# Another place for the keys' and values' group among five gate groups, and context rows eighteen pieces apart

## The chip, the cores and the metric

The kernel runs on one core of one Trainium2 chip. Its engines each have a queue of their own and work through it in order: TensorE (PE) multiplies matrices, VectorE (DVE) and ScalarE (ACT) do arithmetic by element, GpSimd (POOL) does small work and issues DMAs that add to what lies at their target, and SyncE (SP) issues most loads. Engines wait for each other, and for transfers, by semaphores. The metric is device time in microseconds (us), the median of several runs.

## The reference, cut to what matters

One layer of an attention and Fourier block on 512 tokens of width 2048 in float32, with 256 tokens of context. Nearly all time goes into one projection of width 9216 and the output products behind it.

```python
h  = _modulate(_rmsnorm(xs, norm_g[l]), shift[:, None], scale[:, None])   # 512 x 2048
hc = _modulate(_rmsnorm(cs, norm_g[l]), shift_c, scale_c)                 # 256 x 2048
pc_kv = hc @ w_l[:, OFF_K:OFF_ZA]                  # keys and values of the context
kc = _rmsnorm(_heads(pc_kv, 0, N_KV_HEADS), k_norm_g[l])
vc = _heads(pc_kv, KV_W, N_KV_HEADS)
p = h @ w_l                                        # q, k, v, z_a, u_b, z_b, g_a, g_b
q = _rope(_rmsnorm(_heads(p, OFF_Q, N_Q_HEADS), q_norm_g[l]), cos, sin) * q_scale
k = _rope(_rmsnorm(_heads(p, OFF_K, N_KV_HEADS), k_norm_g[l]), cos, sin)
v = _heads(p, OFF_V, N_KV_HEADS)
attn = _attention(q, jnp.concatenate([k, kc], axis=1), jnp.concatenate([v, vc], axis=1))
y = _merge(p[..., OFF_ZA:], attn, w_proj_a[l], w_proj_b[l], w_out[l])
#   in _merge:  y_a = (attn * silu(z_a)) @ w_pa,  y_b = (fourier(u_b) * silu(z_b)) @ w_pb
#               (sigmoid(g_a) * y_a + sigmoid(g_b) * y_b) @ w_out
out = _rmsnorm(xs + gate[:, None] * y, final_g)
```

## The kernel before, in words

**Groups.** Eight groups of 1024 columns of the projection run one after the other: three groups of queries and z (`qz`), two gate groups, the group of the keys and values (`kv`, number `KV` = 5), two more gate groups. The gate groups compute the sigmoids of g_a and g_b and store them (L813, L814). The list `KINDS` names them, and the host lays the columns of `w_g` out in that order. The keys' group also multiplies the context, so it is longer than the others. After the eighth group come attention, the two branch projections and the output projection.

**Products and pieces.** Each group is computed as a two by two block product in Winograd's manner, with seven products in place of eight, in the order P1, Q5, P2, Q6, P7, Q3, Q4. A product has four pieces (P2.0 to P2.3). A piece is 128 x 1024 raw weights (512 KB). To keep float32's precision every factor is split in a high and a low part: `hi` is a copy rounded by ACT (L163), `lo` is the difference formed by DVE (L164). Three matmuls (L305 to L307: hi by hi, hi by lo, lo by hi) replace one, which gives twelve matmuls of 512 columns for each piece.

**Sums of weights.** Products Q5, Q6, and Q4 need sums of the four quarters of a group's weights, piece by piece. Four buffers R0 to R3, one for each piece, hold them: SP loads the first quarter (L205), DVE adds the second for Q5 (L250), and POOL issues DMAs that add the third and the fourth (L261), each as soon as the split that reads the buffer is done. P7 needs the sum less a quarter, which DVE subtracts into the raw buffer (L252) in the time of the products ahead.

**Buffers.** Raw weights are loaded (L202) into four buffers of one pool and up to two more (`raw0`, `raw1`). Split weights go into three pairs of `hi`, `lo`, and two more pairs on the place of x's halves (their rows read `s33`, `s35`, `s63`, `s65`, and so on, in halves of 512 columns), which are given up for the end of the group ahead of the keys' and come back in the group behind it. From the seventh group on two further raw buffers, `gvp`, open where `qr` lay. `qr` holds what the rotation and transposition of queries and keys (L860 to L872) writes, the stores of the queries (L899, `q_d`) and of the keys (L912, `k_d`) read, and the context's rows use in between. L215 loads queries back for attention.

**Context.** The context's norm is formed in the first gate group: `context_spread` needs L987. Then its rows are normalised, modulated and brought into the seven forms of the products in four blocks (L1002 to L1011, then ACT, then a store, `cr` pieces). Each block takes one raw buffer, and stands at a fixed place in the sequence of pieces, counted from the first gate group.

**Order.** The program is written in the order of the products, a piece splits several pieces ahead, and pieces are loaded as far ahead as buffers allow. A scheduler then orders each engine's queue by when it deems work ready. Thus a change of places in the lists also changes which of two instructions stands first on DVE or SP.

Of the kernel before, what the change touches and what calls it, by code (L numbers as in the profile page):

```python
# [33 lines left out]
O_Q, O_K, O_V, O_ZA, O_UB, O_ZB, O_GA, O_GB, IN_W = 0, 1536, 2048, 2560, 4096, 4608, 5120, 7168, 9216  # L34
# [20 lines left out]
BY_DVE_GATES, BY_DVE_OUT = (1,), ()  # L55


KINDS = ("qz", "qz", "qz", "gate", "gate", "kv", "gate", "gate")
NQZ, KV = 3, 5
LAST = len(KINDS) - 1  # L60

CTX_FORMS = ("A11", "Z5", "A12", "A22", "S3", "S2", "S4")
# [2 lines left out]
def context_piece(g, name, pc):  # L65

    n = 28 * (g - NQZ) + 4 * ONE_GROUP.index(name) + pc
    if n % 2 == 0 and 0 <= n < 8:
        return "cn", n // 2
    if n % 10 == 4 and 14 <= n < 54:  # L70
        return "cr", n // 10 - 1

# [33 lines left out]
def block_kernel(ctx, tc, xT, ctx_rows, ctx_toks, x, c_row, w_ss, w_gate, vecs, qkg, rope, dft_c, dft_s,  # L108
# [4 lines left out]
    def region(name, side="left", **kw):  # L113
        st = ExitStack()
        return st, st.enter_context(tc.tile_pool(name=name, bufs=1, side=side, **kw))
# [596 lines left out]
    def job():  # L712
        if late:
            late.pop(0)()
        if jobs:
            jobs.pop(0)()
# [93 lines left out]
    def gate_done(half, c, v, t):  # L810
        t = new_ev() if t is None else t
        g = KINDS[: group.g].count("gate")
        nc.scalar.activation(t, v, ACT.Sigmoid)  # L813
# [8 lines left out]
    def load_rotations(rows):  # L822
        nc.scalar.dma_start(turning, rope)
        nc.scalar.dma_start(new_q()[:, 0, 0:2, :], rows)

    def rotations(factor):
        r, gq = turning, new_q()[:, 0, 0:2, :]
        for a in range(2):
            nc.vector.scalar_tensor_tensor(r[:, a], r[:, a], factor,
                                           gq[:, None, a, :].broadcast_to([P, 4, HD]), op0=ALU.mult, op1=ALU.mult)  # L830
# [213 lines left out]
    qz, qs, kv = {}, {}, {}  # L1044

    def load_head(h):
        qz[h] = take((2, T))
        nc.gpsimd.dma_start(qz[h][:, 1, :], flat(z_d[h]))
        load_turned(qz[h][:, 0, :], q_d[h // 4], h % 4)

    def get_keys(g):
        keys = get(("K", g))
        kv[g] = tuple(w[:, 0, :] for w in keys) + get(("V", g))

    def split_queries(h):
        qs[h] = take((2, T), F32R)
        split_from(qz[h][:, 0, :], qs[h][:, 0, :], qs[h][:, 1, :])

    load_rotations(qkg[:, 0:2, :])
    for g, kind in enumerate(KINDS):  # L1060
        if g == 3:
            jobs += [lambda: None] * 8 + [context_norm, lambda: None, lambda: None, context_spread]
        elif g == KV:
            while jobs:
                job()
            assert not any(p[2] == "raw1" for e in ahead for p, _ in e.raws)
        elif g == KV + 1:
            hl_pools += range(MORE_HL)
        group = Group(g, forms, new_ev, {"qz": qz_done, "kv": kv_done, "gate": gate_done}[kind], {"a": "x", "b": "y", "c": "x"})
        if g == KV:  # L1070
            group.more = Context()
        for name in ONE_GROUP:
            if (g, name) == (0, "Q5"):
                hl_pools += range(MORE_HL)
                rotations(HD ** -0.5)
            elif (g, name) == (KV, "P1"):
                load_rotations(qkg[:, 2:4, :])
            elif (g, name) == (KV, "Q5"):
                rotations(1.0)
            elif (g, name) == (KV - 1, "Q3"):  # L1080
                raw_pools.remove((rp, 1, "raw1", 1))
                hl_pools[:] = [p for p in hl_pools if not isinstance(p, int)]
            elif (g, name) == (KV + 1, "Q6"):
                qzs.close()
                gvs, gvp = region("gvp", "right", reuse_waits="tile")
                raw_pools += [(rp, 1, "raw1", 1), (gvp, 2, "raw", 2)]
            elif (g, name) == (LAST, "P7"):
                raw_pools.pop()
                raw_pools.remove((rp, 1, "raw1", 1))
            elif (g, name) == (LAST, "Q3"):  # L1090

                free += [(fms[i], f"s{i}") for i in (4, 5, 6, 7, 12, 13, 14, 15, 8, 9, 10, 11, 2, 3, 0, 1)]
                for h in range(2):
                    load_head(h)
            elif (g, name) == (LAST, "Q4"):
                hl_pools[:] = [p for p in hl_pools if not isinstance(p, int)]
                get_keys(0)
                jobs.append(lambda: split_queries(0))
            group.run(name)
# [429 lines left out]
def _constants():  # L1529
    pos = np.arange(T)  # L1530
    inv = (THETA ** (-np.arange(32, dtype=np.float64) / 32)).astype(np.float32)
    ang = np.stack([(pos // GRID).astype(np.float32)[:, None] * inv,
                    (pos % GRID).astype(np.float32)[:, None] * inv], axis=1)
    ang = ang.astype(np.float64)
    cos, sin = np.cos(ang), np.sin(ang)
    cos = np.stack([cos, cos], axis=2).reshape(T, HD)
    sin = np.stack([-sin, sin], axis=2).reshape(T, HD)
    rope = np.stack([cos, sin]).reshape(2, 4, P, HD).transpose(2, 0, 1, 3).astype(np.float32)
    a = 2 * np.pi * (np.outer(np.arange(P), np.arange(P)) % P) / P
    dft_c = np.concatenate([np.cos(a), -np.sin(a)], axis=1).astype(np.float32)  # L1540

    f = np.concatenate([np.arange(0, T, 2), np.arange(1, T, 2)])
    a = 2 * np.pi * (np.outer(np.arange(T // 2), f) % T) / T
    dft_s = np.stack([np.cos(a), np.sin(a)]).reshape(2, 2, P, T).transpose(2, 0, 1, 3).reshape(P, 2, 2 * T).astype(np.float32)
    return np.ascontiguousarray(rope), np.ascontiguousarray(dft_c), np.ascontiguousarray(dft_s)


def _layout(x, c, ctx, c_ctx, w_ada, b_ada, norm_g, w_in, q_norm_g, k_norm_g, w_proj_a, w_proj_b, w_out, final_g):
    A = lambda v: np.ascontiguousarray(v)
    x, ctx, w_ada, w_in = (np.asarray(v)[0] for v in (x, ctx, w_ada, w_in))  # L1550
    w_pa, w_pb, w_o = (np.asarray(v)[0] for v in (w_proj_a, w_proj_b, w_out))
    col = lambda v: np.asarray(v).reshape(KK, P).T
    rope, dft_c, dft_s = _constants()
    d = {}
    d["xT"] = A(x.T.reshape(KK, P, T).transpose(1, 0, 2))

    d["ctx_rows"] = A(ctx.T.reshape(2, 4, 2, P, C).transpose(1, 3, 0, 2, 4).reshape(4, P, 4 * C))
    d["ctx_toks"] = A(ctx.reshape(2, P, 2, 1024).transpose(0, 2, 1, 3).reshape(4, P, 1024))
    wk = w_ada.reshape(KK, P, 3, KK, P)
    d["w_ss"] = A(wk[:, :, :2].transpose(3, 1, 0, 2, 4).reshape(KK, P, KK, 2 * P))  # L1560
    d["w_gate"] = A(w_ada[:, 2 * D :].reshape(2, 1024, KK, P).transpose(0, 2, 3, 1).reshape(2 * KK, P, 1024))
    d["c_row"] = A(np.asarray(c))
    b = np.asarray(b_ada)[0]
    vecs = [np.asarray(c)[0], c_ctx, b[:D], b[D : 2 * D], b[2 * D :], np.asarray(norm_g)[0]]
    d["vecs"] = A(np.concatenate([col(v) for v in vecs], axis=1))
    g = [np.asarray(q_norm_g)[0], np.asarray(k_norm_g)[0]]
    sw = lambda v: v.reshape(2, 2, 32)[:, ::-1].reshape(HD)
    rows = np.stack([g[0], sw(g[0]), g[1], sw(g[1])])
    d["qkg"] = A(np.broadcast_to(rows[None], (P, 4, HD)))
    d["rope"], d["dft_c"], d["dft_s"] = rope, dft_c, dft_s  # L1570

    w3 = w_in.reshape(KK, P, IN_W)
    cols = lambda kb, nk, o, n: w3[kb : kb + nk, :, o : o + n].transpose(1, 0, 2)
    d["w_start"] = A(np.concatenate(
        [np.concatenate([cols(kb, nk, o, P) for o in START[t : t + nt]], axis=2).reshape(-1)
         for _, _, kb, nk, t, nt in start_pieces()]))

    def chunks(w):
        w = w.reshape(8, 2, P, -1, 512).transpose(3, 0, 2, 1, 4)
        return w.reshape(w.shape[0], 8, P, 1024)  # L1580


    blocks = lambda w: A(chunks(w).reshape(-1, 2, 2, 4, P, 1024).transpose(0, 2, 1, 3, 4, 5))
    heads = [w_in[:, o + 512 * i : o + 512 * i + 512] for i in range(NQZ) for o in (O_Q, O_ZA)]
    d["w_g"] = blocks(np.concatenate(heads + [w_in[:, O_GA:O_GB], w_in[:, O_K:O_ZA], w_in[:, O_GB:]], axis=1))
    d["w_pab"] = A(chunks(np.concatenate([w_pa, w_pb], axis=0)))
    d["w_o"] = blocks(w_o)
    d["x"] = A(x.reshape(2, 2, P, 4, 512).transpose(0, 3, 2, 1, 4))
    d["final_g"] = A(np.asarray(final_g)[None])
    return d  # L1590
# [15 lines left out]
```

## Time and profile before

| What | Value |
| --- | --- |
| median of 3 runs | 1329.95 us (1327.25 to 1331.77) |
| profiled execution: its time, its span | 1326.24 us, 1324.5 us |
| PE busy | 1291.6 us, 98% of the span, 6522 matmuls |
| DVE busy | 983.3 us, 74% |
| ACT busy | 657.0 us, 50% |
| POOL busy | 136.4 us, 10% |
| DMA | 291.28 MB, mean 220 GB/s |

A span is the time from the first to the last recorded instruction. A row of a timeline has the start in us, the duration in us, the engine, the line, the operation with output and inputs, and in brackets the idle time ahead of it with what ended it. PE's matmuls overlap, so the pace is the distance from one start to the next. In a table by windows each engine's busy time is followed by its number of instructions; the last three columns are the mean granted clock, the share of time that the DMA engines are busy, and GB/s. "DMA to landing" is the time from the issue of a transfer to its completion.

### The profile page before, as it was taken

To read this page: it belongs to the slowest core of one execution; us is meant where nothing else is said; L and a number is where in the kernel's file an instruction comes from. 1 tells how busy PE (TensorE), PEld (TensorE's weight loads), DVE (VectorE), ACT (ScalarE), POOL (GpSimd) and SP (SyncE) were. 2 spreads that over 40 slices of the span, in tenths; PEclk is the share of its full clock that TensorE was granted. 3 is DMA by queue.
4 is the path that set the end of the run, shared out by engine and by line. 5 is a ranking of instruction groups with operands and counts; after the bars stand their busy time and mean duration, and the time that the engine had idled before them with its cause. 6 is when DMAs were issued, how large, how long until landed. Compare 5 with 4: busy or idle time off the path is not lost. (4 is left out here: it accounts for less than half of the span.)

```text
span 1324.5 us, 17511 instructions
## 1 busy us (share of the span) xinstructions
PE 1291.6 (98%) x6522; PEld 1053.6 (80%) x6522; DVE 983.3 (74%) x1341; ACT 657.0 (50%) x1018; POOL 136.4 (10%) x186
## 2 busy tenths in 40 slices
PE   7999999999999999999999999999999999999995
PEld 3566888888888887888888888888888888878884
DVE  4655889878777875748487667778776889687677
ACT  5322655555555553544354545767665133364534
POOL 1110011110201111011021010000000100110210
PEclk9999999999999999999999999999999999999999
DMA  9996677887898987977659798432113988778973
GB/s 382 404 383 250 222 194 204 217 231 214 198 306 214 280 275 199 306 180 171 203 153 329 226 220 211 100 90 80 33 49 128 350 346 301 185 155 252 225 204 127
DMA packets 125718, 291.28 MB, mean 220 GB/s; under 512 B 46784, under 2 KB 60608, under 8 KB 121280
## 3 DMA queue, kind: packets, MB, share of 16 engines
q1 hardware_dynamic: 88912, 176.10, 39.7%
q0 software_dynamic: 21168, 91.24, 28.6%
q10 hardware_dynamic: 15552, 22.81, 4.9%
q8 instruction: 51, 0.84, 0.3%
q14 instruction: 35, 0.29, 0.1%
HBM read 263.37 MB, written 26.75 MB: 219 GB/s over the span
## 5 line engine op out<-in xcount | busy, mean ns | idle before, releaser
L163 ACT ACTIVATE whi<-wr 128x1024 fp32r<-128x1024 f32 (+1 forms) x129 | 135.1, 1052 | 180.2 <-PE y L307 77.3
L306 PE MATMUL x<-wlo,s 128*128 128x512 f32 x548 | 214.4, 391 | 4.0 <-DVE wlo L164 4.0
L305 PE MATMUL y<-whi,s 128*128 128x512 f32 x544 | 214.3, 394 | 1.8 <-ACT s L774 1.1
L305 PE MATMUL x<-whi,s 128*128 128x512 f32 x548 | 214.6, 392 | 0.2 <-ACT s L771 0.2
L307 PE MATMUL x<-whi,s 128*128 128x512 f32 x548 | 214.0, 391 | 0.0
L306 PE MATMUL y<-wlo,s 128*128 128x512 f32 x544 | 212.3, 390 | 1.3 <-DVE wlo L164 1.3
L307 PE MATMUL y<-whi,s 128*128 128x512 f32 x544 | 212.3, 390 | 0.0
L164 DVE TENSOR_TENSOR wlo<-wr,whi 128x1024 fp32r<-128x1024 f32 (+1 forms) x129 | 155.6, 1212 | 63.4 <-ACT whi L163 63.0
L163 ACT ACTIVATE whi<-R 128x1024 fp32r<-128x1024 f32 x115 | 121.2, 1059 | 129.5 <-PE x L307 58.5
L164 DVE TENSOR_TENSOR wlo<-R,whi 128x1024 fp32r<-128x1024 f32 x115 | 140.0, 1221 | 48.7 <-ACT whi L163 48.5
L306 PEld LDWEIGHTS x<-wlo,s 128*128 128x128 f32 x548 | 103.2, 188 | 26.3 <-DVE wlo L164 5.1
L305 PEld LDWEIGHTS y<-whi,s 128*128 128x128 f32 x544 | 102.2, 188 | 24.4 <-DVE s L1200 2.8
L305 PEld LDWEIGHTS x<-whi,s 128*128 128x128 f32 x548 | 103.3, 189 | 22.1 <-ACT s L771 0.5
L307 PEld LDWEIGHTS x<-whi,s 128*128 128x128 f32 x548 | 103.2, 188 | 21.5
L307 PEld LDWEIGHTS y<-whi,s 128*128 128x128 f32 x544 | 102.1, 188 | 21.6
L306 PEld LDWEIGHTS y<-wlo,s 128*128 128x128 f32 x544 | 102.2, 188 | 20.5 <-DVE wlo L164 1.7
L306 PE MATMUL x<-s,s 128*128 128x512 f32 (+1 forms) x284 | 106.7, 376 | 0.0
L307 PE MATMUL x<-s,s 128*128 128x512 f32 (+1 forms) x284 | 105.9, 373 | 0.0
L305 PE MATMUL x<-s,s 128*128 128x512 f32 (+1 forms) x274 | 104.0, 379 | 0.9 <-ACT s L1160 0.9
L261 POOL DMA_DIRECT2D R<-in_w_g x64 | 55.4, 865 | 435.0 <-DVE wlo L164 319.2
L163 ACT ACTIVATE s<-wr 128x512 fp32r<-128x512 f32 (+2 forms) x98 | 64.3, 679 | 52.7 <-PE y L306 14.0
L164 DVE TENSOR_TENSOR s<-wr,s 128x512 fp32r<-128x512 f32 (+2 forms) x98 | 71.2, 752 | 20.9 <-ACT s L163 19.9
(274 smaller groups left out, 2246.0 us busy)
## 6 DMA issues: line engine op xcount, KB each, us to landing
wr<-in_w_g SPq DMA_DIRECT2D x128, 512.0 KB, 4.7
R<-in_w_g POOLq DMA_DIRECT2D x64, 512.0 KB, 7.0
wa<-in_w_ss POOLq DMA_DIRECT2D x28, 1024.0 KB, 9.1
R<-in_w_g SPq DMA_DIRECT2D x32, 512.0 KB, 5.1
wr<-in_w_pab SPq DMA_DIRECT2D x32, 512.0 KB, 5.0
wr<-in_w_gate SPq DMA_DIRECT2D x32, 512.0 KB, 5.4
wr<-in_w_o SPq DMA_DIRECT2D x24, 512.0 KB, 5.4
R<-in_w_o POOLq DMA_DIRECT2D x24, 512.0 KB, 7.4
```

The lines of the kernel that those rows point to most:

```text
L163: nc.scalar.activation(hi, src, ACT.Copy)
L164: return nc.vector.tensor_tensor(lo, src, hi.bitcast(F32), op=ALU.subtract)
L261: nc.gpsimd.dma_start(chain[e.pc], e.nxt, accum_op=ALU.add)
L305: nc.tensor.matmul(o, ah, bh, start=start, stop=False, skip_group_check=cont)
L306: nc.tensor.matmul(o, ah, bl, start=False, stop=False, skip_group_check=cont)
L307: nc.tensor.matmul(o, al, bh, start=False, stop=stop, skip_group_check=cont)
```

## The change

The keys' and values' group moves from place 5 to place 6 of the eight: three gate groups stand ahead of it and one behind it. Its columns move accordingly in `w_g`. The context's four blocks of rows stood at pieces 14, 24, 34 and 44, counted from the first gate group, and stand at 16, 34, 52 and 70. All that hangs on `KV` moves with it: the rotations' loads, the removal and return of the two extra pairs of split weights and of `raw1`, and the context's forms. The two buffers `gvp` open in the group behind the keys, as before, but ahead of its second product instead of ahead of its fourth.

```diff
-KINDS = ("qz", "qz", "qz", "gate", "gate", "kv", "gate", "gate")
-NQZ, KV = 3, 5
+KINDS = ("qz", "qz", "qz", "gate", "gate", "gate", "kv", "gate")
+NQZ, KV = 3, 6
...
-    if n % 10 == 4 and 14 <= n < 54:
-        return "cr", n // 10 - 1
+    if n % 18 == 16 and 0 <= n < 72:
+        return "cr", n // 18
...
-            elif (g, name) == (KV + 1, "Q6"):
+            elif (g, name) == (KV + 1, "Q5"):
                 qzs.close()
                 gvs, gvp = region("gvp", "right", reuse_waits="tile")
                 raw_pools += [(rp, 1, "raw1", 1), (gvp, 2, "raw", 2)]
...
-    d["w_g"] = blocks(np.concatenate(heads + [w_in[:, O_GA:O_GB], w_in[:, O_K:O_ZA], w_in[:, O_GB:]], axis=1))
+    d["w_g"] = blocks(np.concatenate(heads + [w_in[:, O_GA : O_GB + 1024], w_in[:, O_K:O_ZA], w_in[:, O_GB + 1024 :]], axis=1))
```

How it moves instructions is shown at three places. In the rows R0_1233 to R3_1236 are the four sums (pieces 0 to 3), `wr` are raw weights and `wlo`, `whi` their split parts.

**DVE, first gate group, ahead of the transposition of the last queries.** A piece of the difference, with the rows of before as - and those of the change as +:

```order
 L164 TENSOR_TENSOR s_451<-R_1235,s_450 128x2x256
 L164 TENSOR_TENSOR s_585<-R_1235,s_584 128x2x256
+L252 TENSOR_TENSOR wr_3511<-R_1233,wr_3511 128x1024
 L860 TENSOR_TENSOR y_3316<-ev_2911,qr 128x8x32 x2
+L164 TENSOR_TENSOR wlo_3424<-R_1236,whi_3423 128x1024
 L865 TENSOR_TENSOR y_3316<-qr,y_3316 128x1024
-L164 TENSOR_TENSOR wlo_3424<-R_1236,whi_3423 128x1024
 L872 STREAM_TRANSPOSE qr<-y_3316 128x1024
 L164 TENSOR_TENSOR wlo_3432<-wr_3420,whi_3431 128x1024
```

The P7 subtraction on R0 now stands ahead of the rotation (L860, L865) and of the transposition; the split of the fourth piece of P1 (from R3) changes places with L865. A little further on, the subtraction on R2 now stands ahead of the split of Q6.0 (from R0) instead of behind it:

```order
 L987 TENSOR_SCALAR qr<-ident,small 128x128
-L252 TENSOR_TENSOR wr_3529<-R_1233,wr_3529 128x1024
 L164 TENSOR_TENSOR s_451<-wr_3465,s_450 128x2x256
 L164 TENSOR_TENSOR s_585<-wr_3465,s_584 128x2x256
 L252 TENSOR_TENSOR wr_3547<-R_1234,wr_3547 128x1024
-L252 TENSOR_TENSOR wr_3586<-R_1236,wr_3586 128x1024
-L164 TENSOR_TENSOR wlo_3493<-R_1233,whi_3492 128x1024
-L252 TENSOR_TENSOR wr_3568<-R_1235,wr_3568 128x1024
+L252 TENSOR_TENSOR wr_3592<-R_1236,wr_3592 128x1024
+L252 TENSOR_TENSOR wr_3572<-R_1235,wr_3572 128x1024
+L164 TENSOR_TENSOR wlo_3491<-R_1233,whi_3490 128x1024
 L164 TENSOR_TENSOR wlo_3514<-R_1234,whi_3513 128x1024
```

Q6.0's split is the row that reads R_1233.

**DVE, second gate group, around the splits of P2.** The rows `wlo` from `wr` are P2.1 to P2.3 (P2.0 is the pair s86, s110 ahead of them); s35 and s65 from R3 are Q5.3. Before:

```order
L164 TENSOR_TENSOR wlo533_3954<-R2_1235,whi532_3953 128x1024
L164 TENSOR_TENSOR s35_228<-R3_1236,s33_227 128x2x256
L1011 SCALAR_TENSOR_TENSOR qr_1569<-qr_1569,shift_99 128x128
L252 TENSOR_TENSOR wr546_4097<-R0_1233,wr546_4097 128x1024
L164 TENSOR_TENSOR s65_347<-R3_1236,s63_346 128x2x256
L1009 TENSOR_TENSOR small_95<-shift_99 128x1 x2
L164 TENSOR_TENSOR s86_451<-wr531_3950,s84_450 128x2x256
L164 TENSOR_TENSOR s110_585<-wr531_3950,s108_584 128x2x256
L252 TENSOR_TENSOR wr557_4174<-R3_1236,wr557_4174 128x1024
L164 TENSOR_TENSOR wlo539_4024<-wr536_4003,whi538_4023 128x1024
L164 TENSOR_TENSOR wlo542_4042<-wr537_4021,whi541_4041 128x1024
L164 TENSOR_TENSOR wlo544_4064<-wr540_4039,whi543_4063 128x1024
```

In the change:

```order
L164 TENSOR_TENSOR wlo532_3934<-R2_1235,whi531_3933 128x1024
L164 TENSOR_TENSOR s35_228<-R3_1236,s33_227 128x2x256
L252 TENSOR_TENSOR wr545_4077<-R0_1233,wr545_4077 128x1024
L164 TENSOR_TENSOR s65_347<-R3_1236,s63_346 128x2x256
L164 TENSOR_TENSOR s86_451<-wr530_3930,s84_450 128x2x256
L164 TENSOR_TENSOR s110_585<-wr530_3930,s108_584 128x2x256
L164 TENSOR_TENSOR wlo538_4004<-wr535_3983,whi537_4003 128x1024
L164 TENSOR_TENSOR wlo541_4022<-wr536_4001,whi540_4021 128x1024
L252 TENSOR_TENSOR wr546_4095<-R1_1234,wr546_4095 128x1024
L164 TENSOR_TENSOR wlo543_4044<-wr539_4019,whi542_4043 128x1024
L164 TENSOR_TENSOR s35_228<-R0_1233,s33_227 128x2x256
L252 TENSOR_TENSOR wr549_4113<-R2_1235,wr549_4113 128x1024
```

Two subtractions, on R0 and R3, stood ahead of the last three P2 splits. Now one, on R0, stands ahead of P2.0's, and another, on R1, ahead of P2.3's alone; the one on R3 is further behind.

**SP and DVE, the group behind the keys' group.** SP's loads of raw weights in the first products of that group, before:

```order
L202 DMA wr689_5375<-in_w_g 128x1024
L202 DMA wr692_5393<-in_w_g 128x1024
L202 DMA wr709_5548<-in_w_g 128x1024
L202 DMA wr693_5411<-in_w_g 128x1024
L202 DMA wr697_5447<-in_w_g 128x1024
L202 DMA wr706_5528<-in_w_g 128x1024
L202 DMA wr700_5465<-in_w_g 128x1024
L202 DMA wr703_5483<-in_w_g 128x1024
L202 DMA wr705_5508<-in_w_g 128x1024
L202 DMA wr712_5568<-in_w_g 128x1024
L202 DMA wr717_5592<-in_w_g 128x1024
```

and in the change, where wr747 and wr748 are the raw weights of P2.2 and P2.3, and `s783`, `s784` take queries for attention:

```order
L202 DMA wr756_5973<-in_w_g 128x1024
L202 DMA wr759_5991<-in_w_g 128x1024
L202 DMA wr746_5885<-in_w_g 128x1024
L202 DMA wr762_6009<-in_w_g 128x1024
L202 DMA wr764_6030<-in_w_g 128x1024
L215 DMA s783_6190<-q_d_77 32x16x32 x2
L202 DMA wr765_6050<-in_w_g 128x1024
L202 DMA wr768_6070<-in_w_g 128x1024
L215 DMA s783_6190<-q_d_77 32x16x32
L202 DMA wr747_5887<-in_w_g 128x1024
L202 DMA wr748_5889<-in_w_g 128x1024
L215 DMA s783_6190<-q_d_77 32x16x32
```

The loads of P2.2 and P2.3 now go into the `gvp` buffers; they stand behind five loads that are needed later and behind three of the queries' loads. DVE in the same place, from the transposition of the keys (L872), before:

```order
L872 STREAM_TRANSPOSE qr_1569<-y681_5278 128x1024
L164 TENSOR_TENSOR wlo691_5378<-wr689_5375,whi690_5377 128x1024
L164 TENSOR_TENSOR s35_228<-wr692_5393,s33_227 128x2x256
L164 TENSOR_TENSOR s65_347<-wr692_5393,s63_346 128x2x256
L164 TENSOR_TENSOR s86_451<-wr693_5411,s84_450 128x2x256
L164 TENSOR_TENSOR s110_585<-wr693_5411,s108_584 128x2x256
L252 TENSOR_TENSOR wr697_5447<-R0_1233,wr697_5447 128x1024
L164 TENSOR_TENSOR wlo696_5432<-R0_1233,whi695_5431 128x1024
L252 TENSOR_TENSOR wr700_5465<-R1_1234,wr700_5465 128x1024
L164 TENSOR_TENSOR wlo699_5450<-R1_1234,whi698_5449 128x1024
L252 TENSOR_TENSOR wr703_5483<-R2_1235,wr703_5483 128x1024
L164 TENSOR_TENSOR wlo702_5468<-R2_1235,whi701_5467 128x1024
```

and in the change:

```order
L872 STREAM_TRANSPOSE qr_1569<-y740_5800 128x1024
L164 TENSOR_TENSOR wlo752_5908<-wr746_5885,whi751_5907 128x1024
L252 TENSOR_TENSOR wr756_5973<-R0_1233,wr756_5973 128x1024
L252 TENSOR_TENSOR wr759_5991<-R1_1234,wr759_5991 128x1024
L252 TENSOR_TENSOR wr762_6009<-R2_1235,wr762_6009 128x1024
L164 TENSOR_TENSOR wlo755_5958<-R0_1233,whi754_5957 128x1024
L252 TENSOR_TENSOR wr764_6030<-R3_1236,wr764_6030 128x1024
L164 TENSOR_TENSOR wlo758_5976<-R1_1234,whi757_5975 128x1024
L164 TENSOR_TENSOR wlo761_5994<-R2_1235,whi760_5993 128x1024
L164 TENSOR_TENSOR s35_228<-wr747_5887,s33_227 128x2x256
L164 TENSOR_TENSOR s65_347<-wr747_5887,s63_346 128x2x256
L164 TENSOR_TENSOR s86_451<-wr748_5889,s84_450 128x2x256
```

The splits of P2.2 and P2.3 (s35, s65 from wr747 and s86, s110 from wr748) stood directly behind those of P2.0 and P2.1. Now four subtractions and the splits of Q6.0 to Q6.2 (from R0, R1, R2) stand ahead of them.

## The prediction, made before the changed kernel ran

> **What bounds the kernel now.** I read the page first, then the waits of the matrix engine, then the timelines of the two places where a wait stands or will stand. The page and the timeline of PE at its normal pace (first row and the row 56 matmuls later):
>
> ```profile
> span 1324.5 us, 17511 instructions
> PE 1291.6 (98%) x6522; PEld 1053.6 (80%) x6522; DVE 983.3 (74%) x1341; ACT 657.0 (50%) x1018; POOL 136.4 (10%) x186
> ```
> ```profile
> 199.81 0.39 PE L306 MATMUL x<-s,s 128*128 128x512 f32 x1
> ...
> 212.50 0.39 PE L305 MATMUL y<-s,s 128*128 128x512 f32 x1
> ```
>
> PE is the bound: 98% busy, one matmul every 12.69/56 = 0.227 us, so a piece of weights (12 matmuls) is 2.72 us, a product (4 pieces) 10.9 us, a gate group 76 us. The change alters no matmul. It can only remove or add time in which PE stands still. Between 195 and 800 us, the whole stretch of the eight groups, the waits of PE are one line:
>
> ```profile
> PE x L306 <- DVE wlo L164: 2.9, 1, 2.9
> ```
>
> Its surroundings on PE:
>
> ```profile
> 505.55 0.50 PE L306 MATMUL x<-wlo,s 128*128 128x512 f32 x1 [2.85 <-DVE wlo L164]
> ...
> 506.72 0.63 PE L307 MATMUL x<-whi,s 128*128 128x512 f32 x1
> 507.14 0.63 PE L305 MATMUL x<-whi,s 128*128 128x512 f32 x1
> ...
> 509.70 0.47 PE L305 MATMUL x<-whi,s 128*128 128x512 f32 x1
> 510.01 0.40 PE L306 MATMUL x<-wlo,s 128*128 128x512 f32 x1
> ```
>
> This is P2.1 of the second gate group. PE idles 2.85 us and then pays again: from 505.55 to 510.01 twelve matmuls take 4.46 us, not 2.72, because from 506.7 to 509.7 they come every 0.43 us, half speed. Together 2.85 + 1.74 = **4.6 us**. That is all the change can win in the groups. Who was late, on DVE:
>
> ```profile
> 493.30 1.23 DVE L252 TENSOR_TENSOR wr<-R,wr 128x1024 f32<-128x1024 f32 x1 [4.45 <-DMA wr<-in_w_g]
> 494.44 0.69 DVE L164 TENSOR_TENSOR s<-R,s 128x512 fp32r<-128x512 f32 x1
> ...
> 503.13 1.23 DVE L252 TENSOR_TENSOR wr<-R,wr 128x1024 f32<-128x1024 f32 x1 [6.66 <-DMA R<-in_w_g]
> 504.27 3.49 DVE L164 TENSOR_TENSOR wlo<-wr,whi 128x1024 fp32r<-128x1024 f32 x3
> ```
>
> Two P7 subtractions (L252) stand early in DVE's row. The first waits 4.45 us for its raw weights, whose slot a context row had held; that delays the second half of Q5.3 (494.44), so the accumulating DMA on R3 starts late, and the second L252 waits 6.66 us for it. The three low parts that P2 needs stand behind it.
>
> **The gain, -4.6 us.** In the change the subtraction on R3 stands behind all four P2 splits, and the context row that held the slot is finished earlier. P2.1's low part (needed at 505.55 - 2.85 = 502.7) now follows P2.0's directly: even with the 4.45 us wait kept it ends near 496.4 + 1.1 = 497.5. What stands ahead of a P2 part is now the subtraction on R1, ahead of P2.3 alone. Its raw load goes into the slot that P2.1's split frees, about 497.6. With 6.1 to 10.3 us for a load (rows below) it lands by 504 to 508, P2.3 is split 2.3 us later, and is needed at 508.1: hidden by two more pieces of matmuls, at worst 2 us late. I take the whole 4.6.
>
> **First gate group, +0.8 us.** A P7 subtraction moves up there, ahead of the transposition of the last queries:
>
> ```profile
> 411.23 0.90 DVE L860 TENSOR_TENSOR y<-ev,qr 128x256 f32<-128x256 f32 x2
> ...
> 414.44 1.25 DVE L872 STREAM_TRANSPOSE qr<-y 128x1024 f32<-128x1024 f32 x1
> ...
> 422.62 0.29 DVE L987 TENSOR_SCALAR qr<-ident,small 128x128 f32<-128x128 f32 x1 [5.83 <-DMA q_d<-qr]
> 422.82 1.22 DVE L164 TENSOR_TENSOR wlo<-wr,whi 128x1024 fp32r<-128x1024 f32 x1
> ...
> 430.98 1.22 DVE L164 TENSOR_TENSOR wlo<-R,whi 128x1024 fp32r<-128x1024 f32 x1
> 432.30 1.23 DVE L252 TENSOR_TENSOR wr<-R,wr 128x1024 f32<-128x1024 f32 x1
> ```
> ```profile
> L261 POOL DMA_DIRECT2D R<-in_w_g x4: 839/892/923, 407.2 to 414.8; - x4
> ...
> DMA to landing us min/median/max: 5.3/6.2/7.5
> ```
> ```profile
> L899 ACTq DMA_DIRECT2D q_d<-qr x2: 339/423/507, 415.7 to 416.1; - x2
> ...
> DMA to landing us min/median/max: 6.8/7.2/7.7
> ```
> ```profile
> 434.03 1.03 ACT L813 ACTIVATE ev<-x 128x1024 f32<-128x1024 f32 x1 [0.73 <-PE x L307]
> ```
>
> R0's accumulation, issued at 407.2, lands no sooner than 412.5, and the subtraction takes 1.13, so the two L860 start at 413.6 instead of 411.23, 2.4 us later, and so do the transposition, its store, and DVE's wait at 422.62. Q6.0's split (430.98) now stands behind the subtraction that followed it at 432.30: with the same loads it starts 432.30 + 1.13 + 2.4 = 435.8 less about 1.2, since that subtraction now waits for its raw alone, and ends at 435.7. PE needs it at about 434.3, as the second matmul of Q6 or the next, since Q6 starts where P2 ends, and the sigmoid that reads P2 starts at 434.03. So 1.4 us late if the store takes 6.8 us again; nothing if it takes what the same store took in the group before:
>
> ```profile
> L899 ACTq DMA_DIRECT2D q_d<-qr x2: 326/396/467, 372.9 to 373.3; - x2
> ...
> DMA to landing us min/median/max: 2.0/2.2/2.5
> ```
>
> I take 0.8; bounds 0 and 1.4.
>
> **Third gate group, +0.3 us.** It is new in this place and has two context rows' work less far apart than a group. The subtraction on R3 stands ahead of P2.2, one piece (2.72 us) later than in the stall above. The same waits would leave 2.85 - 2.72 = 0.1 us. If its load takes 10.3 us (the longest below) in place of 6.7, it is 3.7. I take 0.3; bounds 0 and 3.7.
>
> **The group behind the keys and values, +8.7 us.** Here the change adds a wait. The two spare buffers share their place with qr, which the keys' stores (L912) still read. Before, their first loads served Q3, far ahead. Opened at Q5 in the only group left, they serve P2.2 and P2.3. The group behind the keys, now:
>
> ```profile
> 692.70 1.24 DVE L872 STREAM_TRANSPOSE qr<-y 128x1024 f32<-128x1024 f32 x1
> 693.87 1.18 DVE L164 TENSOR_TENSOR wlo<-wr,whi 128x1024 fp32r<-128x1024 f32 x1
> ```
> ```profile
> L912 ACTq DMA_DIRECT2D k_d<-qr x2: 339/426/514, 694.5 to 694.9; - x2
> ...
> DMA to landing us min/median/max: 8.8/9.5/10.3
> ```
> ```profile
> L202 SPq DMA_DIRECT2D wr<-in_w_g x2: 328/376/425, 705.3 to 705.6; - x2
> ...
> DMA to landing us min/median/max: 6.1/8.2/10.3
> ```
> ```profile
> L202 SPq DMA_DIRECT2D wr<-in_w_g x3: 328/328/328, 424.1 to 427.8; - x3
> ...
> DMA to landing us min/median/max: 3.6/4.4/4.4
> ```
> ```profile
> 704.90 0.63 ACT L163 ACTIVATE s<-wr 128x512 fp32r<-128x512 f32 x1 [0.78 <-PE x L307]
> 706.21 1.03 ACT L813 ACTIVATE ev<-x 128x1024 f32<-128x1024 f32 x1 [0.68 <-PE x L307]
> ```
> ```profile
> 684.00:718.00 34.00, 34.00 (x151) 28.16 (x150) 27.98 (x32) 19.64 (x28) 8.10 (x9) 1.00 1.03 284
> ```
>
> DVE's order up to the transposition is the same in the change, so I use these times as its clock. P2 ends at 706.2, so P2.2 starts two pieces earlier, 700.7. In the change PE first does eight matmuls of Q6.0 (1.8 us) and at 702.5 needs the high part of P2.2. The stores, issued at 694.5 and 694.9, land at 703.3 and 705.2. SP issues the two loads at 705.3 and 705.6, and the first lands at 711.4. A half on ACT takes 0.63: 712.0, or **9.5 us late**. In the change ACT can issue the stores 0.6 us sooner (693.9), and of the raw loads ahead of them two have gone; two z loads and pieces of q_d come instead. DMA is full there (share 1.03). Waiting behind these loads are ACT's and DVE's next rows (they are in order) and SP's q_d pieces, which nobody needs before attention. The lower bound is 0: a store in 2.0 us (above) and a load in 4.4 (the first group's row) land in time. A second limit: P2.2's low part stands behind two Q6 splits and the subtraction on R3. R3's accumulation:
>
> ```profile
> L261 POOL DMA_DIRECT2D R<-in_w_g x4: 862/895/928, 682.9 to 690.8; - x4
> ...
> DMA to landing us min/median/max: 6.8/9.5/12.0
> ```
>
> Issued at 690.8 and landing at 702.8, it puts the low part at 702.8 + 3 x 1.13 + 0.6 = 706.8, against a need at 702.5 + 6 x 0.227 = 703.9: 2.9 us late by itself, inside the first wait. I take 7.0 us, nearer the upper bound because the same two DMAs were measured in the same place; and after a stall this long the half-speed stretch, 1.7 us as measured at 506.7.
>
> On that stretch the Trainium skill, TensorE: Matmul & The Clock Gate, section What's actually happening, says that the clock falls to half after at least one idle window of about 3.4 us. The trace has it fall after only 2.85, so the measurement decides. By the page alone a wait under 3.4 us would cost no stretch, and the sum would be 1.7 us less if this wait stayed so short.
>
> **Sum.** -4.6 + 0.8 + 0.3 + 7.0 + 1.7 = **+5.2 us**. The profiled execution took 1326.2 us for its span of 1324.5, so it would take 1331.4. The median shown, 1329.95, lies 3.7 above that execution; I forecast 1335 for a median.
>
> **Rivals.** About 0.3%, 4 us, is what can be told from no change here.
> (a) Forecast, 55%: the late spare buffers cost more than the stall removed; +2 to +8, 1332 to 1338.
> (b) Partly covered, 22%: stores and loads hurry, only the order on DVE is left (0 to 2.9 us); -4 to +1, 1326 to 1331. For it: fewer loads in flight. Against: DMA share 1.03.
> (c) Faster, 10%: the wait behind the keys does not appear at all. It decides on the landing of the keys' stores: landed by 697.5 in the clock above (3.6 us after the transposition), a 4.4 us load is in time, PE stays fed, and the 4.6 us stand: 1325. For it: the queries' stores in an emptier stretch took 2.0. Against: all four landings quoted here took 6.8 or more.
> (d) Worse, 9%: the short covers in the first and third gate groups add their upper bounds, 1.4 and 3.7, and the spare load the full 9.5: +12, 1342.
> (e) The change does not do what it says, 4%: the stall at P2.1 stays for another reason, and the rest comes on top: +9.8, 1340.
>
> **Numbers.** Over 4 us slower: most of (a) (0.42), (d) and (e), and 0.03 of (b): 0.58. Within 4 us: 0.13 of (a), 0.16 of (b), 0.01 of (c): 0.30. Faster: 0.09 of (c), 0.03 of (b): 0.12. The range 1328 to 1341 leaves out (c), the end of (b) and part of (d). The forecast's own range is 1332 to 1338.
>
> **What would show it.** Right: PE's waits have no line near 505 us; a new one of 5 to 9 us near 716 us, in P2 of the last gate group, on ACT's split of raw weights or the load behind it, then eight matmuls at half speed; SP's waits have the keys' store (k_d from qr) ahead of it. Wrong if that wait is under 3 us, if a stall of several us stands in the first or third gate group, or if the one at P2.1 of the second stays.

## The result and the profile after

The changed kernel takes 1345.41 us (median of four runs, 1343.36 to 1350.38) against 1328.6 (four runs, 1325.29 to 1331.77): a ratio of 1.0126, 95% interval 1.0103 to 1.0149. It is 16.8 us slower. The forecast was 1335, with a range from 1328 to 1341, so the sign was right and the size was not. Of all executions in this document one, of the rows seventeen apart, ran at a granted clock of 0.82 (1479.31 us), and it is left out.

The busy times of the changed kernel, and the waits of PE between 190 and 830 us (columns: who waited for whom, us in total, times, the longest):

```profile
PE 1292.5 (96%) x6522; PEld 1055.0 (79%) x6522; DVE 984.1 (73%) x1340; ACT 657.3 (49%) x1017; POOL 136.0 (10%) x186
```
```profile
PE x L305 <- ACT s L163: 13.6, 1, 13.6
PE x L306 <- DVE s L164: 3.7, 1, 3.7
```

PE does the same 6522 matmuls and is busy 1292.5 us, against 1291.6; what grew is the time in which it stands still. The one line of before, 2.9 us on `wlo`, is gone, and two others are there. Where they are, on PE's timeline, with the ends of the half-speed stretches behind them:

```profile
587.02 0.75 PE L306 MATMUL x<-s,s 128*128 128x512 f32 x1 [3.73 <-DVE s L164]
...
590.77 0.39 PE L306 MATMUL x<-s,s 128*128 128x512 f32 x1
```
```profile
794.65 0.79 PE L305 MATMUL x<-s,s 128*128 128x512 f32 x1 [13.58 <-ACT s L163]
...
799.16 0.39 PE L305 MATMUL x<-s,s 128*128 128x512 f32 x1
```

The first is P2 of the third gate group, the second P2.2 of the last. From 587.02 to 590.77 nine steps take 3.75 us in place of 9 x 0.227 = 2.04: 1.7 more. From 794.65 to 799.16 eleven steps take 4.51 in place of 2.50: 2.0 more. So the two stalls cost 3.7 + 1.7 = 5.4 and 13.6 + 2.0 = 15.6, and the old one (4.6) is gone: +16.4. The profiled execution took 1343.36, 17.1 more than the one of before. The remaining 0.7 lies mostly outside these groups: by PE's starts, the same matmul near 190 us stands 1.6 us later, and 1.3 are won back from 830 us to PE's last matmul. The times of the two profiles thus differ by 1.6 us already where the gate groups begin.

What made the last group wait: the keys' stores and the two late raw loads, from the groups of DMA issues, then ACT's split that waited for the first of them, and the engines in the stretch of the loads (PE, PEld, DVE, ACT, POOL busy with counts, granted clock, DMA share, GB/s):

```profile
L912 ACTq DMA_DIRECT2D k_d<-qr x2: 338/425/512, 772.5 to 772.9; - x2
...
DMA to landing us min/median/max: 7.5/8.4/9.3
```
```profile
L202 SPq DMA_DIRECT2D wr<-in_w_g x2: 327/384/440, 782.4 to 782.7; - x2
...
DMA to landing us min/median/max: 11.6/12.2/12.8
```
```profile
793.97 1.15 ACT L163 ACTIVATE s<-wr 128x512 fp32r<-128x512 f32 x2 [13.61 <-DMA wr<-in_w_g]
```
```profile
782.30:794.00 11.70, 0.00 (x0) 0.00 (x0) 0.75 (x1) 0.04 (x1) 1.64 (x2) 0.62 1.09 282
```

The loads start 0.1 us after the second store landed (772.9 + 9.3 = 782.2), when PE has already stood for 1.3 us (its last matmul started at 780.68). The first then takes 11.6 us, in which the engines do next to nothing (DVE 0.75 us, POOL 1.64) and the DMA engines are full (share 1.09).

### The profile page after: what moved, and what is told of

It is laid out like the page before. It is cut to its first block, busy times and chain, and to the rows that moved or that the text cites. A ratio compares the mean times of both kernels' runs of the same rounds, so it can differ in the third digit from the quotient of the medians.

```text
span 1341.6 us, 17506 instructions
## 1 busy us (share of the span) xinstructions
PE 1292.5 (96%) x6522; PEld 1055.0 (79%) x6522; DVE 984.1 (73%) x1340; ACT 657.3 (49%) x1017; POOL 136.0 (10%) x186
## 5 line engine op out<-in xcount | busy, mean ns | idle before, releaser
L305 PE MATMUL x<-s,s 128*128 128x512 f32 (+1 forms) x272 | 104.3, 384 | 14.7 <-ACT s L163 13.6
```

The costliest lines, as they stand in the source:

```text
L305: nc.tensor.matmul(o, ah, bh, start=start, stop=False, skip_group_check=cont)
```

## The experiments

**The spare buffers' opening put back.**

```diff
-            elif (g, name) == (KV + 1, "Q5"):
+            elif (g, name) == (KV + 1, "Q6"):
```

> The change with one line taken back: the two spare buffers open ahead of the fourth product of the group behind the keys, as before, not ahead of the second. Theory A (late buffers): the 13.6 us wait in P2 of the last group, with its half-speed stretch some 15.9 us, is the wait of two raw loads for the keys' stores; with ordinary buffers for P2 it goes, the rest stays, so 1345.4 - 15.9 = 1329.5, with the new 3.7 us wait in the third gate group still there. Rival B (order and traffic): VectorE's order in that place and the crowded DMA make P2 late whatever buffer it uses; then a wait of 6 us or more stays there and the time is 1336 or more.

Measured: 1333.83 us (ratio to before 1.0038, 1.0022 to 1.0055; before 1329.23 on that chip). PE's waits:

```profile
PE x L306 <- DVE s L164: 3.4, 1, 3.4
PE x L306 <- DVE wlo L164: 2.3, 2, 1.5
PE y L306 <- DVE wlo L164: 2.1, 2, 1.8
```

The wait of 13.6 us is gone: theory A. The gain is 11.6 by medians instead of 15.9, and the time 4.3 above the forecast of 1329.5. This profile is of the slowest of the ten executions (1337.42). It has 2.3 us of small waits in the second and third gate groups (near 548 and 582 us) that the changed kernel's profile has not, though in both kernels every engine does the same work in the same order up to 768 us. So these waits differ from one execution to another, and the edit did not make them. New behind the edit are 2.1 us (`y`, near 794 us) in Q6 of the last group, which are taken up again below. How much of either is in the median is not shown.

**The same line alone, in the kernel before.**

```diff
-            elif (g, name) == (KV + 1, "Q6"):
+            elif (g, name) == (KV + 1, "Q5"):
```

> The kernel before with one line of the change alone: the spare buffers open ahead of the second product of the group behind the keys, which is there the seventh of eight, with no queries' loads near. Theory A: P2.2 waits for the keys' stores and a load there too: the stores land near 703 to 705, the load takes 6 to 10 us, against a need at 702.5: a wait of 7 to 11 us and 1.7 of half speed, 1328.6 + 9 to 13 = 1338 to 1341. If the crowd of queries' and z loads of the last group is the larger part of the wait, it is under 5 us here: 1331 to 1335.

Measured: 1341.04 us (1.008, 1.0058 to 1.0102). PE's waits, and the two loads into the spare buffers:

```profile
PE x L305 <- ACT s L163: 8.8, 1, 8.8
PE x L306 <- DVE wlo L164: 2.5, 1, 2.5
```
```profile
L202 SPq DMA_DIRECT2D wr<-in_w_g x2: 328/426/523, 708.1 to 708.5; - x2
...
DMA to landing us min/median/max: 3.8/4.9/6.0
```

The early opening costs 11.8 us by itself, at the upper end of the forecast. PE starts to wait at 703.75. Of its 8.8 us, 4.3 pass until the loads can start behind the stores (708.1), 3.8 with the load and 0.7 with ACT's split. In the last group it was 1.3, 11.6 and 0.7. So the stores are about half of the wait here and little of it there, and there is something in the last group that slows the load.

**The queries' loads out of the way.**

```diff
-                for h in range(2):
-                    load_head(h)
             elif (g, name) == (LAST, "Q4"):
+                for h in range(2):
+                    load_head(h)
```

> The change with the first two heads' queries and z loads issued one product later (ahead of Q4 instead of Q3), so that none of them is in flight beside the stores of the keys and the two late raw loads. If they made the raw load slow (11.6 us from issue to landing), it now takes 6 to 8 and the wait in the last group falls from 13.6 to 8 to 10 us: 1340 to 1342. If the accumulating loads of the weights' sums made it slow, or the stores set the wait, it stays at 12 us or more and the time at 1344 to 1346.

Measured: 1344.01 us (1.01, 1.0079 to 1.012). PE's waits in this kernel, its two late loads, and its DMA packets between 770 and 796 us; behind them the packets of the changed kernel in the same stretch, with its queries' loads (number, size of one, median us to landing):

```profile
PE x L305 <- ACT s L163: 8.1, 1, 8.1
PE x L306 <- DVE s L164: 3.1, 1, 3.1
PE x L306 <- DVE wlo L164: 2.2, 2, 1.4
PE y L306 <- DVE wlo L164: 0.6, 1, 0.6
```
```profile
L202 SPq DMA_DIRECT2D wr<-in_w_g x2: 328/378/427, 787.0 to 787.4; - x2
...
DMA to landing us min/median/max: 3.6/4.3/5.0
```
```profile
DMA packets 2138, 7.26 MB, mean 279 GB/s; under 512 B 238, under 2 KB 238, under 8 KB 2137
```
```profile
DMA packets 5206, 7.17 MB, mean 276 GB/s; under 512 B 3424, under 2 KB 3424, under 8 KB 5205
...
s<-q_d SPq DMA_DIRECT2D x4, 64.0 KB, 12.6
```

The load falls from 11.6 to 3.6 us and the wait from 13.6 to 8.1, as expected if the queries' and z loads slowed it. The two z loads had landed by 782.2 us in the changed kernel, ahead of the raw loads, which leaves the queries'. They move little (64 KB each), but in packets of 128 bytes: 3424 small packets against 238. Two things stay open. Whether the packets' size or their place in SP's queue does it was not separated. And the edit changes other neighbours too: beside the first raw load two earlier raw loads and three accumulating DMAs of the sums were still in flight in the changed kernel, and two accumulating DMAs here.

The median came down by 1.4 us only, into the band of the other side (1344 to 1346). The profile of this run has 2.8 us of `wlo` waits (`x` and `y`) that the changed kernel's profile does not have, near 536, 548 and 582 us, far ahead of the edit and in the same order of work, as in the first experiment: by PE's starts 3.4 us are lost there and 5.1 won in the last group. The load and the wait themselves are therefore the better measure here.

The Trainium skill, DMA: Bandwidth & Descriptors, section Specifications, says that a transfer needs at least 512 bytes to run at line rate. No run here times such a transfer by itself. What the two profiles show is a neighbour: a 512 KB load took three times as long where the 128-byte packets were in flight.

**The rows' spacing put back.**

```diff
-    if n % 18 == 16 and 0 <= n < 72:
-        return "cr", n // 18
+    if n % 10 == 4 and 14 <= n < 54:
+        return "cr", n // 10 - 1
```

> The change with the context's rows put back ten pieces apart (14, 24, 34, 44); the order of groups and the early spare buffers stay. Theory C (the rows' spacing alone decides where P2 stalls): the wait of 2.85 us in P2 of the second gate group comes back (4.6 us with its stretch) and the 3.7 us wait in the third gate group (5.6 with its stretch) goes; the wait in the last group stays at 12 to 14 us: 1345.4 - 5.6 + 4.6 = 1344.4. Rival D (the third gate group stalls because it now stands directly ahead of the keys' group): that wait stays and the old one is back too, 1350.

Measured: 1346.08 us (1.0112, 1.009 to 1.0133). PE's waits:

```profile
PE x L305 <- ACT s L163: 14.0, 1, 14.0
PE x L306 <- DVE wlo L164: 5.7, 2, 5.3
PE y L306 <- DVE wlo L164: 0.9, 1, 0.9
```

The stall in P2 of the second gate group is back (5.3 us, in an execution of 1351.66, the slowest of four) and the one in P2 of the third is gone (0.9 left there, on `y`, ahead of P2). Theory C holds: the spacing of eighteen did not remove the stall, it moved it by a group.

**The order of the groups alone** (rows ten apart, spare buffers late, both as before):

```diff
-KINDS = ("qz", "qz", "qz", "gate", "gate", "kv", "gate", "gate")
-NQZ, KV = 3, 5
+KINDS = ("qz", "qz", "qz", "gate", "gate", "gate", "kv", "gate")
+NQZ, KV = 3, 6
```

> The order of the groups alone: three gate groups, the keys' group, one gate group, with the rows ten pieces apart and the spare buffers opened late, both as before. If moving the group costs nothing by itself, it is the kernel before: the stall of 2.5 to 5 us in P2 of the second gate group and none over 2 us elsewhere, 1329 to 1332. If the place of the keys' group costs by itself (the last gate group runs into the loads for attention), a wait over 2 us stands in the last group: 1332 to 1336.

Measured: 1333.66 us (1.0032, 1.0015 to 1.0049; before 1329.27). PE's waits, and on DVE the wait behind one of them:

```profile
PE x L306 <- DVE wlo L164: 4.8, 1, 4.8
PE y L306 <- DVE wlo L164: 3.2, 4, 1.2
```
```profile
789.87 1.23 DVE L252 TENSOR_TENSOR wr<-R,wr 128x1024 f32<-128x1024 f32 x1 [7.60 <-DMA wr<-in_w_g]
791.01 1.22 DVE L164 TENSOR_TENSOR wlo<-R,whi 128x1024 fp32r<-128x1024 f32 x1
```

Beside the old stall there are four small ones, two of them in Q6 of the last group: a P7 subtraction ahead of Q6's split waits 7.6 us for its raw load. The time is 4.4 us above before by medians. In the profile 3.2 are these waits, and the old stall is larger too, 4.8 against 2.9. The forecast of no cost fell, but no single new wait is over 2 us, as the other side had it.

**Other spacings.** With the groups in the new order, spare buffers late, rows at 14, 31, 48 and 65:

```diff
-    if n % 18 == 16 and 0 <= n < 72:
-        return "cr", n // 18
+    if n in (14, 31, 48, 65):
+        return "cr", (14, 31, 48, 65).index(n)
```

> The change with the spare buffers opened late (as in the first run of these) and the context's rows at pieces 14, 31, 48 and 65 instead of 16, 34, 52 and 70. Theory C: the stall in P2 depends only on which instructions the rows push ahead of P2's splits on VectorE, so a spacing of which no subtraction with a late load stands ahead of them leaves no wait over 1 us between 190 and 830 us: 1329.2 - 4.6 = 1324.6. Rival D (two gate groups with rows and the keys' group directly behind them cost a wait whatever the spacing): a wait of 2 us or more stays in the second or third gate group: 1328 to 1334.

Measured: 1327.01 us (0.9975, 0.9966 to 0.9985), the median of ten executions without the one of 1479.31, 2.4 us behind the forecast. That one is the profiled execution, so no waits are read from it. The kernel was run again:

> The same kernel as the run with rows seventeen apart, whose profiled execution ran at a granted clock of 0.82 and shows no stall as others have it. Asked: where the 2.5 us lie by which it was behind the forecast of 1324.6. Theory E (the place of the keys' group costs): waits of 1 to 2 us in Q6 of the last group near 792 to 796 us, behind subtractions whose loads are slow beside the queries' loads, as the run with the groups alone showed them (1.2 and 0.6). Rival: they lie in the first 190 us or behind 830 us, which the change does not touch.

Measured: 1327.32 us (0.9989, 0.997 to 1.0008; before 1329.07). PE's waits, and those of DVE between 770 and 800 us:

```profile
PE y L306 <- DVE wlo L164: 2.3, 3, 1.7
```
```profile
DVE wr L252 <- DMA wr<-in_w_g: 9.5, 3, 8.3
```

No wait is left on `x`, where P2 is summed; what is left is mostly Q6 of the last group (1.7 us at 785.33), behind a subtraction that waits 8.3 us for its load. That is theory E. The test of it, with the queries' loads moved as above:

> Rows seventeen apart, spare buffers late, and the first two heads' queries and z loads issued ahead of Q4 instead of Q3. Theory E: without the queries' loads the raw loads of the last group land in 4 to 8 us instead of 11 to 14, the waits near 792 to 796 us go, and the time is 1.5 to 2.5 below that of rows seventeen apart beside it, about 1324. Rival: the time does not move by more than 1 us, since the queries that now come later cost the first head of attention what was won.

Measured: 1322.82 us (0.9955, 0.9941 to 0.9969), 4.5 below the same kernel with the loads in their old place. PE's waits, and DVE's between 765 and 800 us:

```profile
PE tp L1176 <- ACT s L1160: 0.4, 1, 0.4
PE y L306 <- DVE wlo L164: 0.2, 1, 0.2
```
```profile
DVE wr L252 <- DMA wr<-in_w_g: 4.6, 2, 3.9
```

The wait of 1.7 us is gone, and the longest wait for a raw load falls from 8.3 to 3.9. In the last group PE's starts move up by 2.5 us, as theory E has it, and attention loses nothing by queries that come later. Two parts of the forecast were missed. The raw loads land in 7.3 to 11.9 us, against 9.5 to 14.5 with the queries' and z loads beside them, and not in 4 to 8: these loads are a part of the crowd and not all of it. And 4.5 us is more than the 1.5 to 2.5 foretold: from 830 us to PE's last matmul another 3.4 us go, 2.6 of them behind 1200 us. Why, is not shown.

**The groups in their old order, the rows eleven apart.**

```diff
-    if n % 10 == 4 and 14 <= n < 54:
-        return "cr", n // 10 - 1
+    if n in (15, 26, 37, 48):
+        return "cr", (15, 26, 37, 48).index(n)
```

> The kernel before, groups in their old order, with the context's rows at pieces 15, 26, 37 and 48. Theory C: the old stall near 505 us goes without moving any group, 1324.6, with at most a rest of 1 to 2 us in the second gate group, since four rows in two groups stand closer than in three. If only more room between the rows (a third group ahead of the keys) can remove it, the stall stays at 2 us or more: 1328 to 1330.

Measured: 1322.46 us (0.9944, 0.9928 to 0.9959): 6.8 us faster than before, and faster than the change by some 23. PE's waits between 190 and 830 us are one line, and that belongs to attention:

```profile
PE tp L1176 <- ACT s L1160: 0.5, 1, 0.5
```

The stall near 505 us goes without a group being moved. On DVE, at the splits of P2:

```profile
496.35 1.23 DVE L252 TENSOR_TENSOR wr<-R,wr 128x1024 f32<-128x1024 f32 x1 [2.75 <-DMA R<-in_w_g]
...
499.39 1.23 DVE L252 TENSOR_TENSOR wr<-R,wr 128x1024 f32<-128x1024 f32 x1 [1.21 <-DMA R<-in_w_g]
...
501.27 3.49 DVE L164 TENSOR_TENSOR wlo<-wr,whi 128x1024 fp32r<-128x1024 f32 x3
```

Two subtractions still stand ahead of the three low parts. They now wait 2.75 and 1.21 us instead of 4.45 and 6.66, and that is enough. So their place on DVE did not make the stall by itself; how late their transfers landed did. Between 190 and 830 us PE's starts are 5.0 us closer together than before, about the price of the stall; the rest of the 6.8 is not explained. This small edit, and the kernel of the run before it, beat both kernels of this case.

## Why the prediction was right or wrong

The sum was +5.2 us, and the profile has +16.4 in the groups. Of the 11.2 between them the group behind the keys gives 6.9, the third gate group 5.1, and the first gate group -0.8.

**PE bound; the stall near 505 us worth 4.6 us: right.** The DVE timeline of the changed kernel at that place:

```profile
494.34 1.23 DVE L164 TENSOR_TENSOR wlo<-wr,whi 128x1024 fp32r<-128x1024 f32 x1 [0.56 <-ACT whi L163]
497.06 1.23 DVE L164 TENSOR_TENSOR wlo<-wr,whi 128x1024 fp32r<-128x1024 f32 x1 [1.49 <-ACT whi L163]
502.95 1.23 DVE L252 TENSOR_TENSOR wr<-R,wr 128x1024 f32<-128x1024 f32 x1 [4.67 <-DMA wr<-in_w_g]
504.09 1.22 DVE L164 TENSOR_TENSOR wlo<-wr,whi 128x1024 fp32r<-128x1024 f32 x1
```

P2.1's low part is there at 495.6, P2.3's at 505.3 behind the subtraction on R1, whose load landed just ahead of 503. All three came no later than forecast, with the last need at 508 in the clock of before (509.7 here).

**First gate group, +0.8: nothing came, its lower bound.** The rotation moved back by 3.0 us to 414.26, of which 1.6 is the shift of the whole profile; 1.4 are left, and 2.4 were forecast. Q6.0's split came behind three subtractions, but the queries' store landed in 3.8 to 4.8 us instead of 6.8 to 7.7:

```profile
432.37 3.49 DVE L164 TENSOR_TENSOR wlo<-R,whi 128x1024 fp32r<-128x1024 f32 x3
```

Q6.0's low part is ready near 433.6, against a need at 435.9 (434.3 in the clock of before).

**Third gate group, +0.3: the first term that failed; it was 5.4.** The mechanism was the one named, the subtraction on R3 ahead of P2.2's split:

```profile
576.30 1.22 DVE L164 TENSOR_TENSOR wlo<-wr,whi 128x1024 fp32r<-128x1024 f32 x1
...
585.14 1.22 DVE L252 TENSOR_TENSOR wr<-R,wr 128x1024 f32<-128x1024 f32 x1 [6.41 <-DMA wr<-in_w_g]
586.28 1.28 DVE L164 TENSOR_TENSOR s<-wr,s 128x512 fp32r<-128x512 f32 x2
```

The step "the same waits would leave 2.85 - 2.72 = 0.1" took over a wait whose cause was another. Before, the subtraction waited for an accumulating DMA on R3. Now it waits for its own raw weights, whose load could start only when a split freed the slot at 577.5 and landed 7.5 us later. That the wait of 3.7 us equals the upper bound of the text is chance: the bound stood for a load of 10.3 us, and this one took 7.5. The half-speed stretch behind it (1.7) was left out of this term. The runs with other spacings show that the wait depends on the places of the rows. A stall of several us here was one of the text's own signs of being wrong.

**The group behind the keys, +8.7: the second term that failed; it was 15.6.** Stores, loads and ACT's split were the chain forecast, and the wait is where and on what it should be (the "716 us" of the text is not its place in the changed order: a gate group later than 702.5 is near 780). The stores were sized nearly rightly: from the transposition at 771.2 to the landing at 782.2 it was 11.0 us, against 12.5 in the clock of before. What failed was the load: 6.1 us, the faster of two rows measured in the place of before, was used, and the sentence that two z loads and pieces of the queries come "instead" of two raw loads took them as even. The full chain of the text, 9.5 us, less 1.5 for the stores and plus 5.5 for the load, is the 13.6 measured. With the queries' loads issued later the load takes 3.6 us. Without them the waits are 8.1 and 8.8 us, between the 7.0 taken and the upper bound of 9.5. By the prediction's own second limit, the DVE order would have cost 2.9; it never decided.

The half-speed stretch, 1.7 in the sum, was 2.0 in the last group.

**Rivals.** Nearest was (d), the upper bounds together, with 1342 and a chance of 9%: its bounds for the third gate group and the spare load (3.7 and 9.5) were both reached, the second was passed by 4.1, and its 1.4 in the first gate group did not come. Rival (c) was excluded by landings of 7.5 and 9.3 us, as the text weighed it. Landings measured in another neighbourhood had been used as bounds on either side. What was in flight at the new place decided, and the order of SP's queue had shown it (three of the queries' loads stand ahead of the two raw loads).

**Parts of the change.** Against before: the groups' order +4.4, the early buffers +11.8, the spacing nothing that can be told (1333.83 with it, 1333.66 without it, both with the buffers late). In the changed order the early buffers cost 11.6 by medians, too (1345.41 against 1333.83), though PE's wait and stretch there are 15.6 in the profile against 10.9 in the order of before. Where the difference goes is not shown.

## What to carry to other kernels

A buffer that opens earlier is worth nothing if its memory is still being read: find the first user of the new buffers in the order of the queues, and add the landing of the store and of the load before giving it work that is due soon. A load's duration depends on its neighbours (3.6 or 11.6 us here): loads in small packets that a change brings beside it have to be priced from such a place, not counted by bytes. Where work is inserted at fixed places, another spacing may remove the same stall that a larger rearrangement was made for.

## What the runs showed of the hardware that was not expected

PE's half-speed stretch begins after shorter idle times than 2.85 us. In the kernel before with the early buffers a wait of 2.48 us is followed by it; in the first experiment a wait of 1.79 us is not. The same limits hold for all waits in the groups of the profiles compared here, 2.48 us and longer with the stretch, 1.79 and shorter without:

```profile
508.71 0.79 PE L306 MATMUL x<-wlo,s 128*128 128x512 f32 x1 [2.48 <-DVE wlo L164]
509.31 0.63 PE L307 MATMUL x<-whi,s 128*128 128x512 f32 x1
509.73 0.63 PE L305 MATMUL x<-whi,s 128*128 128x512 f32 x1
...
511.80 0.39 PE L307 MATMUL x<-whi,s 128*128 128x512 f32 x1
```
```profile
793.98 0.50 PE L306 MATMUL y<-wlo,s 128*128 128x512 f32 x1 [1.79 <-DVE wlo L164]
794.32 0.40 PE L307 MATMUL y<-whi,s 128*128 128x512 f32 x1
794.55 0.40 PE L305 MATMUL y<-whi,s 128*128 128x512 f32 x1
```

It grows little with the wait: behind 2.5 to 5.3 us of idle time it cost 1.5 to 1.8 more, behind 8.1 to 14.0 us 1.9 to 2.6. The Trainium skill, TensorE: Matmul & The Clock Gate, section What's actually happening, names an idle window of about 3.4 us as the condition; these runs have the half rate after 2.48, so by these rows a wait of 2.5 us is to be counted with some 1.5 us on top.

What stays open: why stores of one size (256 KB, the queries' and the keys') land 2.0 us after their issue in some stretches of a kernel and up to 11.2 in others; and why the profiled executions differ by up to 3.5 us in the first 190 us, which no edit touched.
